# Two rows of one softmax tile loaded through GpSimd in two unequal transfers

## The chip, the cores and the metric

The kernel runs on one core of one Trainium2 chip. The metric is the time of one execution in device microseconds (us); lower is better. A time is compared with that of the kernel before in the same job, on the same chip. Times within the profile count from the span's start; the span is some 1.7 us shorter than the measured time.

## The reference

```python
batch, seq, dim = 16, 1024, 512          # x is float32, 16,384 rows of 512
x_scaled = x / 0.5
exp_x = np.exp(x_scaled - np.max(x_scaled, axis=-1, keepdims=True))
return exp_x / np.sum(exp_x, axis=-1, keepdims=True)
```

It reads 33.55 MB and writes 33.55 MB, and nothing of it is used twice.

## The kernel before

Eight tiles of 128 partitions x 16 rows x 512 (4 MB each, 32 KB per partition) go through six buffers. Sync issues the loads, VectorE (DVE) takes the row maxima and most of the scaling, ScalarE (ACT) the exponentials, two rows' scaling and the stores.

```python
G = 16
WHOLE = [(0, G)]
LOADS = [[(0, 4), (4, G)]] + [WHOLE] * 7
BUFS = 6
...
def load(c):
    if c < BUFS:
        chunks[c] = data.tile([P, G, D], fp32, name="xt")
    else:
        chunks[c] = chunks[c - BUFS]      # tiles 6 and 7 wait for stores 0 and 1
    xt = chunks[c]
    for lo, hi in LOADS[c]:
        nc.sync.dma_start(out=xt[:, lo:hi, :], in_=xr[c][:, lo:hi, :])
...
for i in range(n):
    if i + 1 < n:
        exponentials(i + 1)
    scale_vector(i)
    scale_scalar(i)
    if i + 2 < n:
        shift(i + 2)                      # row maxima; calls load(c)
    store(i)                              # nc.scalar.dma_start, 4 MB
```

Of the kernel before, what the change touches and what calls it, by code (L numbers as in the profile page):

```python
# [1 line left out]

# [4 lines left out]


@with_exitstack
def kernel(  # L10
    ctx: ExitStack,
    tc: tile.TileContext,
    x: bass.AP,
    out: bass.AP,
):
    nc = tc.nc
    fp32 = mybir.dt.float32
    P = nc.NUM_PARTITIONS
    AX = mybir.AxisListType.X
    EXP = mybir.ActivationFunctionType.Exp  # L20
    COPY = mybir.ActivationFunctionType.Copy
    MAX = mybir.AluOpType.max

    D = x.shape[-1]
    xf = x.flatten_outer_dims()
    of = out.flatten_outer_dims()
    N = xf.shape[0]




    G = 16
    C = N // (P * G)
    assert C * P * G == N
    xr = xf.rearrange("(c p g) d -> c p g d", p=P, g=G)
    outr = of.rearrange("(c p g) d -> c p g d", p=P, g=G)
    WHOLE = [(0, G)]
    LOADS = [[(0, 4), (4, G)]] + [WHOLE] * 7
    BLOCKS = [[(0, 4), (4, 8), (8, G)]] + [WHOLE] * 6 + [[(0, 8), (8, G)]]
    STORES = [WHOLE] * 8  # L40
    BMAX = 16
    BUFS = 6

    data = ctx.enter_context(tc.tile_pool(name="data", bufs=BUFS))
    stats = ctx.enter_context(tc.tile_pool(name="stats", bufs=6))

    ctx.enter_context(tc.manual_schedule())


    warm = stats.tile([P, 1], fp32, name="warm", bufs=1)  # L50
    nc.vector.memset(warm, 0.0)  # L51
    nc.scalar.activation(out=warm, in_=warm, func=EXP)  # L52

    chunks = {}
    blocks = [(c, lo, hi) for c in range(C) for lo, hi in BLOCKS[c]]
    n = len(blocks)
    biases, sums, recips = {}, {}, {}
# [5 lines that stand above are left out]
            chunks[c] = chunks[c - BUFS]  # L63
        xt = chunks[c]
        for lo, hi in LOADS[c]:
            nc.sync.dma_start(out=xt[:, lo:hi, :], in_=xr[c][:, lo:hi, :])  # L66

    def shift(i):
        c, lo, hi = blocks[i]
        if c not in chunks:  # L70
            load(c)
        b = hi - lo
        negmax = stats.tile([P, BMAX], fp32, name="negmax")
        nc.vector.tensor_reduce(  # L74
            negmax[:, 0:b], chunks[c][:, lo:hi, :], axis=AX, op=MAX, negate=True
        )
        biases[i] = stats.tile([P, BMAX], fp32, name="bias")
        nc.vector.tensor_scalar_mul(biases[i][:, 0:b], negmax[:, 0:b], 2.0)  # L78

    def exponentials(i):  # L80
        c, lo, hi = blocks[i]
        sums[i] = stats.tile([P, BMAX], fp32, name="sums")
        for g in range(hi - lo):
            row = chunks[c][:, lo + g, :]
            nc.scalar.activation(  # L85
                out=row,
                in_=row,
                func=EXP,
                bias=biases[i][:, g : g + 1],
                scale=2.0,  # L90
                accum_out=sums[i][:, g : g + 1],
            )


    def scale_vector(i):
        c, lo, hi = blocks[i]
        b = hi - lo
        k = b - b // 8
        recips[i] = stats.tile([P, BMAX], fp32, name="recip")
        nc.vector.reciprocal(recips[i][:, 0:b], sums[i][:, 0:b])  # L100
        rows = chunks[c][:, lo : lo + k, :]
        nc.vector.tensor_mul(  # L102
            rows, rows, recips[i][:, 0:k].unsqueeze(2).broadcast_to((P, k, D))
        )

    def scale_scalar(i):
        c, lo, hi = blocks[i]
        b = hi - lo
        for g in range(b - b // 8, b):
            row = chunks[c][:, lo + g, :]  # L110
            nc.scalar.activation(  # L111
                out=row, in_=row, func=COPY, scale=recips[i][:, g : g + 1]
            )

    def store(i):
        c, _, end = blocks[i]
        for lo, hi in STORES[c]:
            if hi == end:
                nc.scalar.dma_start(
                    out=outr[c][:, lo:hi, :], in_=chunks[c][:, lo:hi, :]  # L120
                )

    shift(0)
    shift(1)
    exponentials(0)
# [6 lines that stand above are left out]
            shift(i + 2)  # L132
        store(i)


# [1 line left out]
_INS = ['x']  # L137
_OUTS = [((16, 1024, 512), 'float32')]


# [23 lines left out]
```

## Time and profile before

| | before |
|---|---|
| time, median of 4 runs | 162.23 us (162.18 to 162.25) |
| span in the profile | 160.57 us |
| bytes moved | 67.13 MB, 418 GB/s over the span |
| last store issued | 147.55 us |
| its 16 increments arrive | 158.49 to 158.87 us, one at 159.71 us |

The prediction below shows the page, the windows, the timeline and the chain. Two groups of the page (line, engine, operation, output and input, count; busy time and mean; idle time before) show what DVE does in the span: maxima and scaling, one after the other, with idle time for the first two loads only.

```profile
L74 DVE TENSOR_REDUCE negmax<-xt 128x16 f32<-128x8192 f32 (+2 forms) x11 | 69.9, 6352 | 9.5 <-DMA xt<-in_x_dram 9.5
L102 DVE TENSOR_TENSOR xt<-xt,recip 128x7168 f32<-128x7168 f32 (+2 forms) x11 | 62.0, 5637 | 0.4
```

**The packets, engine by engine.** The views don't name the DMA engine of a packet, and the records don't either; they hold queue, start, duration and size. But the engines can be told apart. On one engine, a packet starts 3 or 4 ns before the recorded end of the one before it, and each transfer from Sync or ScalarE gives each engine eight data packets and then one of 4 bytes, the increment of its semaphore. With these two rules all packets of the kernel before fall into 16 chains, with none left over. I use below: the *lag* of an engine, the start of its last 4-byte packet (of store 7) less the median over the engines; and the *fetch engine*, the chain that holds the two instruction packets of 8,192 bytes. I made this after the prediction, and the chains are my own reconstruction. In the first profile of the change 2 of 2,642 packets are left over, in rows4k, one128_again and half5b1 nine. In half5, later5, early3 and sync_split more are, or the two fetches fall into two chains, and I don't use the chains there.

### The profile page before, as it was taken

The numbers are of one execution on the slowest core, as the hardware profiler recorded it, in microseconds if no ns is written. First come the engines' busy times: TensorE is split into PE (matmuls) and PEld (weight loads), VectorE is DVE, ScalarE is ACT, GpSimd is POOL, SyncE is SP. The second block draws the span as 40 slices with busy tenths as digits, with TensorE's granted clock in tenths as the row PEclk, the third lists the DMA queues.
The fourth block names the chain that finished last, engine by engine and source line by source line (L and its number), as shares of the span: only waits on it lengthen the run. The fifth ranks groups of instructions, "written<-read, shape, count | busy, mean of one in ns | idle before, by whom it ended". The sixth has DMA issues, their size and how long they took to land.

```text
span 160.6 us, 402 instructions
## 1 busy us (share of the span) xinstructions
DVE 134.6 (84%) x45; ACT 102.1 (64%) x273; POOL 0.2 (0%) x4
## 2 busy tenths in 40 slices
DVE  0507999999999999999999999999999999957000
ACT  3071549069979963998199909991899891790000
POOL 0000000000000000000000000000000000000000
DMA  5999999999999999999999999999999999999993
GB/s 182 471 400 506 400 400 498 408 392 484 424 400 384 400 457 449 400 441 465 400 424 473 408 408 492 400 392 498 416 392 490 424 392 457 457 392 449 465 392 139
DMA packets 2450, 67.13 MB, mean 418 GB/s; under 512 B 272, under 2 KB 272, under 8 KB 272
## 3 DMA queue, kind: packets, MB, share of 16 engines
q1 hardware_dynamic: 1296, 33.56, 49.3%
q10 hardware_dynamic: 1152, 33.55, 48.4%
q14 instruction: 2, 0.02, 0.0%
HBM read 33.55 MB, written 33.55 MB: 418 GB/s over the span
## 4 chain that ended last, share of the span: by engine, by line
DVE 80%; DMA 7%; ACT 4%; issue 0%; SPq 0%
DVE negmax L74 42%; DVE xt L102 36%; DMA xt<-in_x_dram 7%; ACT xt L85 4%; DVE bias L78 1%; DVE recip L100 1%; SPq L66 0%
## 5 line engine op out<-in xcount | busy, mean ns | idle before, releaser
L85 ACT ACTIVATE xt<-xt,bias 128x512 f32<-128x512 f32 x128 | 90.4, 708 | 41.7 <-DVE bias L78 41.2
L74 DVE TENSOR_REDUCE negmax<-xt 128x16 f32<-128x8192 f32 (+2 forms) x11 | 69.9, 6352 | 9.5 <-DMA xt<-in_x_dram 9.5
L102 DVE TENSOR_TENSOR xt<-xt,recip 128x7168 f32<-128x7168 f32 (+2 forms) x11 | 62.0, 5637 | 0.4
L85 ACT ACTIVATION_READ_ACCUMULATOR xt<-xt,bias 128x1 f32 x128 | 23.9, 187 | 0.0
L111 ACT ACTIVATE xt<-xt,recip 128x512 f32<-128x512 f32 x15 | 9.9, 706 | 0.0
L100 DVE RECIPROCAL recip<-sums 128x16 f32<-128x16 f32 (+2 forms) x11 | 2.4, 218 | 1.8 <-ACT xt L85 1.8
L78 DVE TENSOR_SCALAR bias<-negmax 128x16 f32<-128x16 f32 (+2 forms) x11 | 1.9, 173 | 0.4
L52 ACT ACT_TABLE_LOAD x1 | 1.3, 1283 | 0.7 <-PEq L148 0.7
L51 DVE MEMSET warm<- 128x1 f32 x1 | 0.1, 59 | 0.8 <-PEq L148 0.8
L52 ACT ACTIVATE warm<-warm 128x1 f32<-128x1 f32 x1 | 0.2, 203 | 0.0
L148 POOL MEMSET const-bfloat16-1.0<- 128x1 bf16 x1 | 0.1, 103 | 0.0
L148 POOL MEMSET const-uint8-127<- 128x1 uint8 x1 | 0.1, 103 | 0.0
L148 POOL MEMSET const-float32-1.0<- 128x1 f32 x1 | 0.1, 100 | 0.0
L148 POOL MEMSET const-float32-0.0<- 128x1 f32 x1 | 0.1, 99 | 0.2 <-issue 0.2
## 6 DMA issues: line engine op xcount, KB each, us to landing
out_dram<-xt ACTq DMA_DIRECT2D x8, 4096.0 KB, 22.8
xt<-in_x_dram SPq DMA_DIRECT2D x7, 4096.0 KB, 30.2
xt<-in_x_dram SPq DMA_DIRECT2D x1, 3072.0 KB, 11.7
xt<-in_x_dram SPq DMA_DIRECT2D x1, 1024.0 KB, 4.9
```

Source lines behind the costliest of these rows:

```text
L51: nc.vector.memset(warm, 0.0)
L52: nc.scalar.activation(out=warm, in_=warm, func=EXP)
L74: nc.vector.tensor_reduce(negmax[:, 0:b], chunks[c][:, lo:hi, :], axis=AX, op=MAX, negate=True)
L78: nc.vector.tensor_scalar_mul(biases[i][:, 0:b], negmax[:, 0:b], 2.0)
L85: nc.scalar.activation(out=row, in_=row, func=EXP, bias=biases[i][:, g : g + 1], scale=2.0, accum_out=sums[i][:, g : g + 1],)
L100: nc.vector.reciprocal(recips[i][:, 0:b], sums[i][:, 0:b])
L102: nc.vector.tensor_mul(rows, rows, recips[i][:, 0:k].unsqueeze(2).broadcast_to((P, k, D)))
L111: nc.scalar.activation(out=row, in_=row, func=COPY, scale=recips[i][:, g : g + 1])
L148: nc = _bacc.Bacc("TRN2", target_bir_lowering=False, num_devices=1)
```

## The change

Its intent, as I read it: the 16 DMA engines are the bound, and one of them is late. Part of one load is moved to GpSimd, whose transfers can be laid on other engines than Sync's, so that the late engine gets less.

```diff
+    SPLIT, TAIL = 6, 2
...
         for lo, hi in LOADS[c]:
+            if c == SPLIT and hi == G:
+                hi = G - TAIL
+                for p0, p1 in ((P - 2, P), (0, P - 2)):
+                    nc.gpsimd.dma_start(
+                        out=xt[p0:p1, hi:G, :],
+                        in_=xr[c][p0:p1, hi:G, :],
+                        max_dma_last_dim=4 * D,
+                    )
             nc.sync.dma_start(out=xt[:, lo:hi, :], in_=xr[c][:, lo:hi, :])
```

## The prediction

> **What bounds the kernel now.** I read the page first, its busy shares and its slices.
>
> ```profile
> DVE 134.6 (84%) x45; ACT 102.1 (64%) x273; POOL 0.2 (0%) x4
> ...
> DVE  0507999999999999999999999999999999957000
> ...
> DMA  5999999999999999999999999999999999999993
> ```
>
> The reader is to see that DVE is busy 84% of the span, but that the DMA row has a 9 in all slices but the first and the last. Then the windows view: busy microseconds of each engine in five stretches, with the busy share and the rate of the 16 DMA engines last.
>
> ```profile
> 0.00:45.60 45.60, 35.03 (x16) 25.09 (x67) 0.20 (x4) 1.00 0.97 414
> 45.60:71.80 26.20, 26.06 (x9) 21.41 (x59) 0.00 (x0) 1.00 1.00 420
> 71.80:115.00 43.20, 42.99 (x12) 31.18 (x85) 0.00 (x0) 1.00 1.01 436
> 115.00:147.60 32.60, 30.52 (x11) 24.43 (x65) 0.00 (x0) 1.00 1.00 433
> 147.60:160.60 13.00, 0.00 (x0) 0.00 (x0) 0.00 (x0) 1.00 0.76 328
> ```
>
> Between 45.6 and 147.6 us the DMA engines have no gap at all: 67.1 MB have to pass, and they pass at some 430 GB/s. Third, the chain of waits and the timeline around the last store (start, length, what).
>
> ```profile
> 137.56 5.76 ACT xt L85 x16
> 143.33 0.02 issue
> 143.35 0.21 DVE recip L100
> 143.56 0.02 issue
> 143.59 3.89 DVE xt L102
> ```
>
> ```profile
> 143.59 3.89 DVE L102 TENSOR_TENSOR xt<-xt,recip 128x3584 f32<-128x3584 f32 x1
> 147.55 0.34 ACTq L119 DMA_DIRECT2D out_dram<-xt  x1
> ```
>
> The last store is issued at 147.55 us. In the trace's packet records the packets of 32,768 bytes take 1.213 us, eight of them per engine and store, so 9.7 us. The first packet of store 7 starts at 148.41 us, 0.86 us after its issue. The last packets of store 6 end between 148.35 and 148.85 us on fifteen engines. So both bounds meet there with a slack of about 0.06 us: DVE delivers the last store just when most engines have finished the one before. Neither a faster DVE nor fewer bytes alone can take much off.
>
> There is one exception, and it is what the change must be about. A DMA's semaphore receives one increment from each of its 16 engines. The increments of store 7 arrive at these times (us from the span's start):
>
> ```
> 158.49 158.51 158.52 158.54 158.55 158.55 158.58 158.62
> 158.66 158.68 158.71 158.75 158.78 158.87 158.87 | 159.71
> ```
>
> Fifteen engines are done by 158.87, one comes **0.84 us later**, and the span ends 0.85 us after that one (160.57). The same late engine shows in stores 4, 5 and 6 (0.93, 0.89 and 0.86 us behind the next). It was not late in the loads of tiles 1 and 2 (the last gap is 0.09 us), and first is, by 0.41 us, in the load of tile 3, which lands at 42.4 us. What came between? The queue lines of the page have it:
>
> ```profile
> q1 hardware_dynamic: 1296, 33.56, 49.3%
> q10 hardware_dynamic: 1152, 33.55, 48.4%
> q14 instruction: 2, 0.02, 0.0%
> ```
>
> The two instruction packets inside the span are of 8,192 bytes and 0.309 us each, at 37.63 and 98.29 us. Some 60 us lie between them, about what ACT needs for 128 instructions, so I take them for ACT's instruction fetch, on one and the same engine. Two by 0.309 is 0.62 us; the 0.84 that is seen, or 1.1 against the middle of the fifteen, is more, so a fetch seems to cost about half a microsecond with what it disturbs. That these fetches are what makes one engine late is my reading; the records name no engine.
>
> **What the Trainium skill says.** "DMA: Bandwidth & Descriptors", section "Issuing engines are not separate DMA queues": transfers from Scalar, Sync and GpSimd run on the same 16 engines and interleave. The trace agrees so far: with loads and stores both in flight the windows show 436 GB/s, and 433 with stores almost alone. So GpSimd brings no bandwidth; it can only move bytes from engine to engine. How, the same page tells in "Why a DMA increments its semaphore by 16 and not by 1": a DMA runs on the largest number of engines up to 16 that divides the slowest dimension; from Sync these are the lowest-numbered ones, from GpSimd a run of consecutive engines from a round-robin cursor. It names an exception: GpSimd gives some direct copies all 16, with a sixteenth of the partitions each, rounded up. Nothing in the trace of before shows either, since all its transfers have 128 partitions. Third, "SWDGE vs HWDGE vs iDMA" on that page: descriptors of GpSimd's transfers are written to rings in SBUF by software. No run here shows that yet; POOL has only four constants in the profile.
>
> **The change part by part.** *Removed from Sync:* the load of tile 6 becomes 14 of 16 rows, so 28,672 bytes per partition. From the packet times (24,576 bytes 0.912 us, 32,768 bytes 1.213 us) that is 36.7 ns per KB, so 1.06 us a packet. Each engine has 8 partitions of it: 8 x 4,096 bytes less, 32,768 bytes, **-1.21 us** per engine.
>
> *Added through GpSimd:* 2 + 126 partitions with 2 rows of 2 KB. By the rule for the number of engines, 2 partitions go on 2 engines, one each, and 126 on 14 engines, nine each. If the cursor starts at engine 0, the small transfer takes engines 0 and 1 and moves the cursor to 2, and the large one takes 2 to 15. This is the only sense I see in loading two partitions first. The bill in bytes: two engines get back 4,096 of 32,768, fourteen get 36,864. So two engines are relieved of 28,672 bytes, 1.06 us, and fourteen have 4,096 bytes, 0.15 us, more. *Smaller rows:* the line through the three packet sizes (8,192 bytes 0.309 us) leaves about 8 ns per packet over the bytes; 18 packets instead of nothing are 0.14 us on the fourteen engines at most.
>
> *Where it falls.* Tile 6's load is issued at 69.38 us, after store 0 has landed, and lands at about 95 us; DVE wants it at 103.94. Nine microseconds are free, so the time GpSimd takes to write some 250 rows' descriptors is hidden, unless it is over that. The DMA engines have work at every moment, so what is taken off the late engine's list comes off its end: in stores 4 to 7 it is behind by the whole of its extra work. DVE gets one or two more waits before one reduction; I book 0.05 us, which the small slack may pass on to the end.
>
> *Sum, if the late engine is one of the relieved two.* Late engine: 159.71 - 1.06 = 158.65, and not before 158.49, which the last issue allows. The fourteen: 158.87 + 0.15 to 0.29 = 159.02 to 159.16. These now end the kernel: 159.71 - 159.1 = 0.6 us gained, 0.1 of which I give back for GpSimd's own waits at the end. From 162.21 that makes 161.6 to 161.7.
>
> **The rivals.** *First: the wrong engine is relieved, or none.* For it: no record names the engine, and the cursor's start is not visible. If the late engine is among the fourteen it gets 0.15 to 0.29 us more, so 162.35 to 162.5. If the exception of the skill holds, eight partitions go on each of 15 engines and six on the last; only if that one is the late one is anything won: 2 x 4,096 bytes, 0.30 us, so 161.9; otherwise 162.2 to 162.35. Against it: a tuned kernel would not have got so odd a shape (2 first, 126 then, one tile out of eight) if it hit nothing.
>
> *Second: DVE becomes the bound.* GpSimd's descriptor writing goes to SBUF while DVE reads and writes there, and any delay of DVE shifts the issue of store 7, where the slack is 0.06 us. For it: DVE has no wait from 33 us to 143 us, so nothing absorbs a delay. Against it: the last fourteen engines begin store 7 up to 0.44 us after the first could, so about 0.3 us of delay is hidden by their own lateness. A DVE delay of 1 us would undo the gain: 162.2 to 162.6.
>
> *Third: the gain is larger since a third queue gets more of the engines.* The windows speak against it: at a DMA share of 1.00 there is no empty time to fill. It would change the order of landing only.
>
> **Range and chances.** I give 60% to the relieved engine being the late one (161.5 to 161.8), 15% to a part of it (161.8 to 162.1), 25% to none or a small loss (162.1 to 162.5). The middle is 161.65, the 80% range 161.4 to 162.4. A gain of 2% would be 3.2 us; the largest lateness to be removed is 0.84 us. A loss of 2% would need a stall of DVE for over 3 us. So 0.01 faster, 0.97 same, 0.02 slower.
>
> **What would show it right or wrong.** Right: the sixteen increments of the last store lie within 0.6 us of each other with no single late one; GpSimd's queue has about 4 + 252 data packets of 2 KB; the increments of GpSimd's large transfer come from 14 engines with the data; store 7 is still issued at 147.5 to 147.7 us. Wrong: one engine still late by 0.8 us or more (rival one), by about 0.5 us (the exception, on the right engine), or all sixteen later because store 7 is issued later (rival two). I would also be wrong if GpSimd's load landed after 104 us, so that the reduction of tile 6 waited.

## The result

The changed kernel takes **162.63 us** (162.61 to 162.72, 4 runs), the one before 162.23 us (162.18 to 162.25). The ratio is 1.0026, with a 95% interval of 1.0009 to 1.0043. (A ratio is the mean time of one kernel's fast runs over that of the other's of the same rounds, so not quite the ratio of the medians.) It is "the same" at the 2% mark, but a loss of 0.4 us where I had expected a gain of 0.6, and outside my range.

The windows of the changed kernel (stretch, its length, busy time and count of DVE, ACT and POOL, clock, DMA share, GB/s):

```profile
0.00:45.60 45.60, 35.01 (x16) 25.09 (x67) 0.20 (x4) 1.00 0.97 413
45.60:71.80 26.20, 26.06 (x9) 21.39 (x59) 0.00 (x0) 1.00 1.01 419
71.80:115.00 43.20, 42.99 (x12) 31.17 (x84) 1.47 (x2) 1.00 1.00 432
115.00:147.60 32.60, 30.54 (x11) 24.45 (x66) 0.00 (x0) 1.00 1.00 430
147.60:160.90 13.30, 0.00 (x0) 0.00 (x0) 0.00 (x0) 1.00 0.81 347
```

The engines are as full as before, but in the two stretches from 71.8 us on they move 432 and 430 GB/s where they moved 436 and 433. That is a coarse sign: the kernel before has 430 in the second stretch too, in its third profile, and a later run without slowed loads (one128_again) has 428 in the first. Nothing below rests on it. DVE is not the cause; the timeline of its last work and of the last store is within 0.03 us of before:

```profile
143.61 3.89 DVE L115 TENSOR_TENSOR xt<-xt,recip 128x3584 f32<-128x3584 f32 x1
147.58 0.34 ACTq L132 DMA_DIRECT2D out_dram<-xt  x1
```

The queue lines now have a fourth queue (packets, MB, share of the engines' span):

```profile
q1 hardware_dynamic: 1296, 33.03, 48.5%
q10 hardware_dynamic: 1152, 33.55, 48.3%
q0 software_dynamic: 192, 0.52, 0.8%
q14 instruction: 2, 0.02, 0.0%
```

The 192 packets are 128 of 4,096 bytes, 32 of 8 bytes and 32 increments. So GpSimd makes packets of 4,096 bytes of the two rows, not rows of 2 KB, and fills the turns of engines without data with 8-byte packets: 14 in the small transfer, 18 (two engines by nine) in the large one. That is 2 and 14 engines with data, as predicted.

By engine, the relief worked: the fetch engine has one data packet from GpSimd where fourteen have nine, and its lag is 0.01 us in place of 1.07. Yet the increments of store 7 arrive like this:

```
158.50 | 158.85 158.88 158.89 158.90 158.94 158.95 158.98 158.99
159.07 159.13 159.17 159.23 159.30 | 159.73 159.89
```

The first is the other relieved engine, which ran 1.4 us ahead and then had to wait for the last store's issue. The rest is later by about 0.4 us, and two other engines are late. The last landing is at 159.89 us in place of 159.71, and from there to the end it takes 1.06 us in place of 0.85. These are the 0.38 us that the span grew (160.57 to 160.95).

### The profile page after: what moved, and what is told of

Same layout as the page of the kernel before. It is cut to its first block, busy times and chain, and to the rows that moved or that the text cites. A ratio compares the mean times of both kernels' runs of the same rounds, so it can differ in the third digit from the quotient of the medians.

```text
span 160.9 us, 410 instructions
## 1 busy us (share of the span) xinstructions
DVE 134.6 (84%) x45; ACT 102.1 (63%) x273; POOL 1.7 (1%) x6
## 4 chain that ended last, share of the span: by engine, by line
DVE 79%; DMA 7%; ACT 4%; issue 1%; SPq 0%
DVE negmax L87 42%; DVE xt L115 36%; DMA xt<-in_x_dram 7%; ACT xt L98 4%; DVE bias L91 1%; DVE recip L113 1%; SPq L79 0%
## 5 line engine op out<-in xcount | busy, mean ns | idle before, releaser
L74 POOL DMA_DIRECT2D xt<-in_x_dram x2 | 1.5, 736 | 71.4 <-DMA out_dram<-xt 71.4
```

What stands on the lines that cost most here:

```text
L74: nc.gpsimd.dma_start(out=xt[p0:p1, hi:G, :], in_=xr[c][p0:p1, hi:G, :], max_dma_last_dim=4 * D,)
```

## The experiments

Two theories went in. **A:** the relief is real, but costs of the GpSimd transfers, and other engines that are late, take its place. **B:** which engine is late is chance, and the fetches have nothing to do with it. The table gathers the runs whose chains I use: data packets that the fetch engine got from GpSimd, its lag, the largest lag of the others, the median engine, the last landing, and the time from it to the end of the span.

| run | fetch engine: packets, lag | others' largest lag | median engine | last landing | to the end |
|---|---|---|---|---|---|
| before | -, 1.07 | 0.24 | 158.29 | 159.71 | 0.85 |
| before_again | -, 1.03 | 0.87 | 158.40 | 159.79 | 0.85 |
| before_third | -, 1.00 | 0.23 | 158.43 | 159.79 | 0.85 |
| changed | 1, 0.01 | 0.93 | 158.62 | 159.89 | 1.06 |
| after_again | 1, -0.53 | 0.24 | 159.07 | 159.79 | 1.05 |
| after_third | 1, -0.01 | 0.23 | 159.15 | 159.86 | 1.06 |
| act_more | -, 1.52 | 0.21 | 158.22 | 160.14 | 0.85 |
| one128 | 8, 1.03 | 0.29 | 158.28 | 159.65 | 0.98 |
| one128_again | 8, 0.92 | 0.26 | 158.60 | 159.86 | 0.97 |
| large_first | 9, 1.59 | 0.29 | 158.64 | 160.59 | 1.05 |
| rows4k | 9, 1.59 | 0.27 | 158.87 | 160.81 | 1.06 |
| tail1 | 5, 1.52 | 0.46 | 158.52 | 160.40 | 1.05 |
| half | 1, 0.40 | 0.56 | 158.85 | 159.89 | 1.06 |
| half5b1 | 1, 0.90 | 0.53 | 158.35 | 159.60 | 1.13 |
| half5b4 | 1, 0.10 | 0.52 | 158.64 | 159.65 | 1.13 |
| tiny | 1, 0.91 | 0.23 | 158.25 | 159.52 | 0.98 |

**1. Both kernels again** (no edit).

> The kernel before, word for word, for a second profile. Theory A (the late engine is the one with the two instruction fetches): in the packet records, put together by engine, the same engine holds both 8,192-byte fetches and ends about 1.07 us behind the median engine; no other is over 0.3 us behind. Theory B (which engine is late is chance, different in each execution): some other engine is late, or the late one holds no fetch. Time 162.2 in both.

> The changed kernel, word for word, for a second profile. In the first one the engine with the fetches was relieved as meant (0.02 us behind the median), but two others were late: one by 0.95 us since the first store began at 47 to 51 us, before GpSimd had moved anything, and one by 0.64 us since GpSimd's transfers at 76 to 103 us. Theory A (the change causes both): both are late again by about as much, and the time is 162.6. Theory B (the first is chance): the engine late since 48 us is missing, or is late by another amount, and the span is some 0.3 us shorter, 162.3, in such an execution. The four times so far (162.61 to 162.72) speak for A.

Measured: 162.48 us (162.32 to 162.91) and 162.67 us (162.43 to 162.74), beside 162.21 us for the kernel before in the same job (162.10 to 162.75 in seven runs). So two sets of runs of the same kernel differ by 0.27 us here, and a difference of that size tells nothing. For the fetch engine my first theory holds: 1.03 us late in the kernel before, and relieved in the change. For the others it does not: in this profile of the change the engine late since 48 us is missing, as theory B of the second expectation has it, and in the kernel before two other engines are late by 0.84 and 0.87 us, since the same moment, when the first store begins. Such lateness is chance and no part of the change. In the kernel before it stays hidden behind the fetch engine.

But the time of the change did not fall with it: the *median* engine ended 0.45 us later than in the first profile. The load packets of tile 6, of 28,672 bytes, took up to 1.22 us in place of 1.06 while GpSimd's packets were in flight (half of them over 1.09 us).

**2. The change a third time.**

> The changed kernel a third time, for another profile: which of the two pictures so far it shows. The engine of the fetches is within 0.1 us of the median or ahead of it in any case. Picture 1: loads not slowed, median at 158.6, one or two engines late by 0.6 to 0.9 us. Picture 2: loads slowed by 0.3 to 0.6 us, median at 158.9 to 159.1, nobody late by over 0.3 us. Both end at 159.7 to 160.0, 162.4 to 162.8.

162.78 us (162.69 and 162.86). Picture 2: loads slowed (up to 1.32 us a packet), nobody late by over 0.23 us. So of three profiles of the change, one has late engines by chance and two have slowed loads. That the sum is about the same each time I take for coincidence; no run tests it. The loss itself came back in every job: 0.40, 0.46 and 0.60 us between the medians.

**3. More instructions for ScalarE.**

```diff
+        if 2 <= i <= 7:                       # after store(i), in the kernel before
+            for _ in range(12):
+                nc.scalar.activation(out=warm, in_=warm, func=COPY)
```

> The kernel before with 72 tiny ScalarE operations added in the idle time of ScalarE (12 after each of six tiles, about 0.2 us each, where it idles 4 us per tile). Theory A (the late engine is late through ScalarE's instruction fetches): three 8,192-byte fetches inside the span in place of two, the second earlier than 98 us, all on one engine, which ends about 1.6 us behind the median in place of 1.05; time up by about 0.5 us, to 162.7 to 162.9. Theory B (the fetches are somebody else's or don't matter): two fetches at 37 and 98 us, the late engine 1.05 us behind, 162.2 to 162.4.

162.76 us (162.68 to 162.84), ratio 1.0031 (1.0016 to 1.0046). The queue line of the page:

```profile
q14 instruction: 4, 0.02, 0.0%
```

One of the four falls at 0.04 us, before any work. The other three are at 37.66, 86.07 and 130.20 us, all in one chain, whose lag is 1.52 us. In the kernel before, 142 ScalarE instructions started between its two fetches; here 151 and 135 between the three, while VectorE's fell from 15 to 11 and 12. The added operations did not delay the last store (issued at 147.44 us). **Theory A holds.** The fetches are ScalarE's, one engine serves them, and the third costs about half a microsecond of the kernel's time, while ScalarE itself has idle time left. The cost is more than the 0.309 us of the packet: the data packet after it is long as well (1.41 to 1.59 us in place of 1.213).

**4. One transfer of 128 partitions.**

```diff
-                for p0, p1 in ((P - 2, P), (0, P - 2)):
+                for p0, p1 in ((0, P),):
```

> The last two rows of tile 6 through GpSimd as one transfer of 128 partitions: the cost of a third queue without the steering. Both theories: 8 data packets of 4,096 bytes on each of 16 engines, nobody relieved. Theory 1 (relief works but is paid for by GpSimd's queue and longer end): the engine with the fetches is late again by about 1.07 us, the end of the program takes 0.2 us longer, so 162.5 to 162.8. Theory 2 (GpSimd's packets cost nothing by themselves; the loss is only the ninth packet of the fourteen engines): 162.2 to 162.35.

> The one transfer of 128 partitions through GpSimd again, for a second profile. Theory 1 (slowed loads are a matter of chance in each execution, whichever way GpSimd's packets are dealt out): load packets of 28 KB at 1.10 to 1.25 us may show this time, with a median engine 0.3 to 0.6 us later. Theory 2 (slowed loads come only where engines hold unequal shares): none again, median at 158.3.

162.50 us (162.41 to 162.66), ratio 1.0012, and 162.60 us in the one look (state unknown, used for its profile). Eight packets on each engine and a fetch engine 1.03 and 0.92 us late: without the unequal shares, no relief. The price that this shows is the end of the program, 0.98 us in place of 0.85. No load packet of tile 6 is slowed in either profile (at most 1.08 us for 28 KB), as theory 2 of the second expectation has it; its 158.3 us for the median engine was a miss, 158.60. There the load packets had already lost some 0.35 us more than in the first profile between 44 and 52 us, before GpSimd moved anything.

**5. The large transfer first.**

```diff
-                for p0, p1 in ((P - 2, P), (0, P - 2)):
+                for p0, p1 in ((0, P - 2), (P - 2, P)):
```

> The 126 partitions first, the two partitions then. If engines are dealt out from a cursor that begins at 0, the large transfer takes the first fourteen engines and the last two are relieved. Theory 1 (the fetch engine is one of the first two, and it was relieved in the change): it now holds nine data packets, is 1.0 to 1.4 us behind the median, and the time is 162.7 to 163.0. Theory 2 (which engines are relieved doesn't matter for the time, the new late engines set it): 162.5 to 162.7, as the changed kernel.

163.48 us (163.41 to 163.67), ratio 1.0075. Theory 1: two other engines are relieved, the fetch engine has nine packets and is 1.59 us late, more than the 1.0 to 1.4 that I had put down, so the time too is above my 162.7 to 163.0. So the order of the two transfers decides who is relieved, and against this order the one in the change is worth 0.8 us.

**6. Without the limit on rows.**

```diff
-                        max_dma_last_dim=4 * D,
```

> The changed kernel without the limit of 2 KB per row, so 4 KB per partition in one row. Theory 1 (the limit doesn't matter: the packets of the change already have 4,096 bytes and take 0.159 us): the same dealing out, 14 engines with 9 packets, 2 with 1, the engine of the fetches relieved, 162.4 to 162.75. Theory 2 (the limit is what makes GpSimd choose 14 engines): all 16 engines hold 8 packets or fewer, the engine of the fetches ends 1 us late, as in the run with one transfer of 128 partitions: 162.4 to 162.7 too, but with the late engine in the records.

163.65 us (163.62 to 163.70), ratio 1.0086. Its queue line:

```profile
q0 software_dynamic: 176, 0.52, 0.8%
```

176 packets are 128 of data, 32 increments and 16 fillers (14 and 2), so the large transfer lay on all 16 engines, eight partitions each and six on one. The fetch engine was not relieved: lag 1.59 us. Load packets of tile 6 were slowed too (half of them over 1.11 us), though all engines had nearly equal shares: unequal shares, theory 2 of one128_again, are not what slows them. Theory 2 was right about the dealing out, and its time was too low. The limit, which I took for a matter of row size, is what makes the change work at all: with it the access has two dimensions behind the partitions, and GpSimd takes 14 engines.

**7. One row, uncut and cut.**

```diff
-    SPLIT, TAIL = 6, 2
+    SPLIT, TAIL = 6, 1          # tail1; half: also max_dma_last_dim=2 * D
```

> One row in place of two, so half the relief. Theory 1 (gain and cost both go with the bytes): the two relieved engines get back about 0.53 us, the fourteen lose about 0.16 in place of 0.33, the engine of the fetches ends 0.3 to 0.5 us behind the median; if no other engine is late by chance, the last landing is at 159.2 and the time 161.9 to 162.1. Theory 2 (the loss comes with the fact of a GpSimd transfer, not with its size): the loads slow down as with two rows, the median engine ends at 158.6 or later, 162.4 to 162.7.

> One row per partition again, but cut into two of 1 KB, so that the access has two dimensions behind the partitions. Theory 1 (two dimensions are what makes GpSimd take 14 engines): 9 partitions on each of 14 engines, the engine of the fetches gets back 0.53 us and is 0.3 to 0.5 us behind the median. Where the loads aren't slowed, the median ends at 158.45 and the time is 161.9 to 162.1; where they are slowed by 0.2 to 0.5 us as in four of the six profiles with GpSimd transfers on tile 6, 162.2 to 162.6. Theory 2 (dealing out is ruled by the bytes): all 16 engines used, the fetch engine late by 1.05 to 1.6 us, 162.5 or more.

tail1 took 162.96 us (162.90 to 163.24) and half 162.71 us (162.26 to 163.12). Their queue lines, tail1 first:

```profile
q0 software_dynamic: 112, 0.26, 0.4%
```

```profile
q0 software_dynamic: 128, 0.26, 0.4%
```

tail1 was meant as half the relief and was none: one row of 2 KB has one dimension, all 16 engines got three to five packets, and the fetch engine was 1.52 us late. half, with the same bytes cut into two of 1 KB, has 14 engines with five packets and two with one, and a lag of 0.40 us, inside the 0.3 to 0.5 expected. Its loads were slowed (up to 1.29 us for 30 KB, that take 1.14), and the median engine ended at 158.85 us; its time is above the 162.2 to 162.6 us of theory 1 for slowed loads. In all, with two GpSimd transfers on tile 6, loads were slowed over all engines in six of seven profiles; with one, in none of two. No run has one transfer of fewer partitions, or two halves of 64, so the number of transfers is not separated from their shape.

**8. The split on tile 3.**

```diff
-    SPLIT, TAIL = 6, 2
+    SPLIT, TAIL = 3, 2
```

> The same split on tile 3, whose load is issued in the first microseconds, when there is no store in flight. Theory 1 (part of the loss comes from the three queues being mixed at 76 to 103 us, where the loads' packets grew from 1.06 to up to 1.2 us in two of three runs): no slow load packets, the median engine ends at 158.6 as the ninth packet alone makes it, the engine of the fetches within 0.3 us of it, last landing about 159.2, 161.9 to 162.2. Theory 2 (the slow loads come from engines that run ahead of the others, whenever that is made): slow load packets here too, 162.4 to 162.7.

164.02 us (163.66 to 164.25), ratio 1.0107. GpSimd's transfers had nothing to wait for and ran from 6.7 to 19.1 us, beside the first loads, whose packets of 24 KB grew from 0.91 to over 1.1 us. The chain of waits, before and then here (start, length, what):

```profile
1.15 11.71 DMA xt<-in_x_dram
```

```profile
1.16 14.48 DMA xt<-in_x_dram
```

DVE started its second block 2.8 us later, with nothing to absorb it, and the last store was issued at 150.32 us. That says little on my two theories (a bad place for the test), but loads beside GpSimd's packets slowed here with no store in flight.

**9. Tile 5, with GpSimd held back.**

```diff
-    SPLIT, TAIL = 6, 2
+    SPLIT, TAIL = 5, 2          # half5...: 5, 1 and max_dma_last_dim=2 * D
...
+                nc.gpsimd.tensor_copy(out=hold, in_=biases[2][:, 0:1])
```

(half5b1 waits for `biases[1]` and half5b4 for `biases[4]`.)

> The split of the change on tile 5, with GpSimd held back by a tiny copy until VectorE has the third block's maxima (22 us), so that its packets meet loads only, no stores, and not the first loads that VectorE waits for. Theory 1 (the loads are slowed only where loads, stores and GpSimd's packets are in flight together): no slow load packets, median at 158.6, fetch engine within 0.1 us of it, 161.9 to 162.3. Theory 2 (GpSimd's packets slow loads wherever they run, as on tile 3): load packets grow from 1.06 and 1.21 us by 5 to 20% for some 12 us, the median engine ends 0.5 to 1 us later, 162.5 to 163.2.

> Half the relief (one row in two of 1 KB) on tile 5, held back in the same way. Theory 1: median at 158.45, fetch engine 0.3 to 0.5 us behind, 161.8 to 162.1: the best of all so far and faster than the kernel before by 0.1 to 0.4 us. Theory 2: loads slowed for the time that GpSimd's packets are in flight, 162.3 to 162.8.

> As the run with half the relief on tile 5, but GpSimd is released by the second block's maxima (15.2 us), so that its packets are done before the first instruction fetch at 37.6 us. In the run before this one the fetch fell into the slowed stretch and the fetch engine ended 0.83 us behind in place of 0.4. Theory 1 (a fetch costs double while the loads are slowed by GpSimd's packets; and half the relief is 0.53 us): the fetch engine is 0.3 to 0.45 us behind, median at 158.4 to 158.6, last landing 159.2 to 159.4, time 161.9 to 162.15. Theory 2 (the lateness there was chance when the first store begins): 162.2 to 162.6.

> The same, but GpSimd is released by the fifth block's maxima (46.2 us), so that its packets run between 49 and 75 us, with loads and stores in flight and no instruction fetch. Theory 1 (what counts is that no fetch meets GpSimd's packets): fetch engine 0.3 to 0.45 us behind, and the median 158.45 plus 0 to 0.5 us for slowed loads: 161.9 to 162.5. Theory 2 (with loads and stores mixed the loads are slowed every time): median at 158.8 or later, 162.3 to 162.6.

Measured: later5 163.21 us (ratio 1.0058), half5 162.37 us (1.0007), half5b1 162.59 us (1.0020), half5b4 162.41 us (1.0006, interval 0.9984 to 1.0028). None is faster than the kernel before. In later5, half5 and half5b1 load packets grew from 1.21 to mostly 1.3 to 1.55 us before any store had begun, as theory 2 has it. In half5 and half5b1 as much came back: in all runs with the split on tile 6 or with none, the median engine's packets lose 0.7 to 1.1 us between 44 and 52 us, when the first store begins; here they lose 0.02. (In later5 too, but there the packets had lost 1.4 us.) half5b1 speaks against my reason: no fetch met GpSimd's packets (19 to 30 us), and the fetch engine was 0.90 us late all the same.

Half a relief lowered the lag by 0.1 us there, by 0.65 in half and by 0.95 in half5b4, but the relief itself is the same in all three: by the chains, the fetch engine's GpSimd packets take 0.60 us less than the median engine's. half5b1 and half5b4 differ in what else the fetch engine lost against the median: by 0.24 us up to 5.2 us, by 0.28 us between 44 and 52 us (in half5b4 it loses 0.29 us less than the median there, in half5b1 no engine loses anything to speak of), and by 0.24 us between 52 and 104 us. Why these losses differ stays open.

half5b4 is the nearest to the aim: fetch engine 0.10 us behind. Even so the last landing came only 0.06 us earlier than before, since another engine was 0.52 us behind, and the end of the program, now with a GpSimd copy in it too, took 1.13 us.

**10. GpSimd's mere presence.**

```diff
+        if c == 6:                             # in the kernel before
+            nc.gpsimd.dma_start(out=scratch[0:2, :], in_=xr[c][0:2, 0, :])
```

> The kernel before with one transfer of 2 rows of 2 KB through GpSimd into a scratch tile that nobody reads: the price of GpSimd's queue being there at all. Theory 1 (the longer end of the program comes with the first GpSimd transfer): 0.95 to 1.06 us from the last landing to the end in place of 0.85, fetch engine 1.05 us behind, 162.3 to 162.5. Theory 2 (it comes from the two extra semaphores and waits of the split): 0.85 us, 162.2.

162.56 us (162.28 to 163.00), a wide spread, ratio 1.0020 (0.9995 to 1.0044), so the time alone tells little. The profile does: 0.98 us from the last landing to the end. One GpSimd transfer costs 0.13 us at the end; the two of the change cost 0.20.

**11. The two rows from Sync.**

```diff
-                for p0, p1 in ((P - 2, P), (0, P - 2)):
-                    nc.gpsimd.dma_start(
+                for p0, p1 in ((0, P),):
+                    nc.sync.dma_start(
```

> Last two rows of tile 6 as a transfer of their own, of 128 partitions, but from Sync. Theory 1 (the slow loads come from GpSimd's queue, not from rows of 28 KB): no slow packets, the end of the program as before (0.85 us after the last landing), the fetch engine 1.05 us behind, 162.2 to 162.35. Theory 2 (packets of 28 KB are slow by themselves): the load packets of tile 6 take 1.1 to 1.2 us, 162.5 or more.

168.23 us (167.95 to 169.38), ratio 1.0382: a miss, and no test of what I had in mind, since it made another wait. Its chain has

```profile
59.02 22.94 DMA out_dram<-xt
...
82.08 45.04 DMA xt<-in_x_dram
```

From Sync the two rows became 256 packets of 2,048 bytes, 16 on each engine, from 74.5 to 92.1 us, ahead of the other fourteen rows in Sync's queue. Each short packet takes its turn against a store's packet of 32,768 bytes. The Trainium skill says that an engine goes round its queues packet by packet ("DMA: Bandwidth & Descriptors", "Queues, rings and completion order"), and this run agrees: in those 18 us the loads got 0.5 MB, store 2 had landed by 92.5 us in place of 108.0, and tile 7 landed at 127.1 us, where DVE had wanted it at 120.6. On a queue of their own, as in the change, such packets held up nobody so: the fourteen rows of tile 6 landed at 94.9 us, as the whole tile did before (95.0).

## Why the prediction was wrong

- **The bound: right.** The DMA engines are full, DVE has no slack, and the last store is issued at 147.58 us after the change. That the fetches make one engine late, which I had only read out of the landings, is shown by act_more.
- **Which engines are relieved: right.** Two engines with one packet, fourteen with nine, and the fetch engine among the two in all three profiles of the change. The first rival (the wrong engine) fell. The skill's exception is real too, and only the limit on rows keeps the change out of it.
- **The relief: right in size.** I had 1.06 us less against 0.15 to 0.29 more for the rest, so a lag of -0.14 to -0.28 from 1.07; measured 0.01, -0.53 and -0.01. Counted in packets it is what I had: the fetch engine's GpSimd packets take 1.20 us less than the nine of the fourteen (booked: 1.06 + 0.15 = 1.21). The scatter of the lag is what else the engine lost or gained against the median.
- **"The fourteen: 158.87 + 0.15 to 0.29 = 159.02 to 159.16. These now end the kernel": this step failed**, in both its terms. *The addend* took the bytes as the only price. The bytes were priced well: on each of the fourteen GpSimd's packets take 1.42 us and the shorter load packets save 1.21, so 0.21 us more. In the first profile the median engine is 0.33 us later than before, close to it. In the other two it is at 159.07 and 159.15 us, against 158.29 to 158.43 in three profiles of before: 0.6 to 0.9 us, since load packets slowed while GpSimd's were in flight (by 0.6 and 0.7 us in sum on the median engine, between 74 and 104 us). I had said in the third rival that a third queue would change the order of landing only; I had not asked whether it changes the pace. *The base*, 158.87, was the end of fifteen engines in one execution. In the first profile of the change another engine was 0.93 us late by chance, as two were in before_again. Behind a fetch engine that is 1 us late, such things cost nothing; without it they are the end.
- **0.1 us for the end: too small.** It is 0.20 us (1.057 less 0.854), and 0.13 of it comes with any GpSimd transfer.
- **The account**, against a predicted last landing of 159.1 us: in the first profile a late engine, in the other two slowed loads, and each time 159.8 to 159.9. With 0.1 more than booked at the end, that is 0.8 to 0.9 us of the 1.0 between predicted and measured time; the rest lies within the spread of the runs.
- **"Nine microseconds are free": held, but only just.** GpSimd's large transfer landed at 103.57, 102.65 and 102.96 us in the three profiles of the change, and DVE began on tile 6 at 103.96, 103.83 and 104.05 us, without a wait. The sign "landed after 104 us" was missed by 0.4 us in the first of them.
- **The second rival** (DVE slowed by GpSimd's descriptors) fell: DVE is busy 134.6 us in both pages.
- **What I named as signs** misled in part: I had promised increments within 0.6 us of each other. They spread over 1.4 us in the first profile, also because the other relieved engine ran ahead. And "4 + 252 data packets of 2 KB" are 128 of 4 KB, so 9 for an engine and not 18. One reading of the landings was off: the 0.93 us are store 3's; stores 4, 5 and 6 have 0.90, 0.90 and 0.86.

What stays open: the mechanism by which GpSimd's packets slow the loads, why a single transfer of 128 partitions did not do it in two profiles while two transfers did in six of seven, and why the fetch engine's other losses differ so much from run to run.

## What to carry to other kernels

Where all engines of a pool are full, the latest one sets the end, so taking work off it wins only the distance to the next latest: look at the second and third over several executions before you count on it. Price a rebalancing by what the extra path does to the pace of all the others, not by its bytes; here a full microsecond of relief was real and was paid back by slower loads, chance lateness and a longer end. A setting that looks like a detail of row size can decide how a transfer is laid on the engines, so check the packet counts of the queues.

## What the Trainium skill lacked or had wrong

- "DMA: Bandwidth & Descriptors", "Why a DMA increments its semaphore by 16 and not by 1": it says that GpSimd gives "some direct copies" all 16 engines but not which. Here 126 partitions with one run each (4 KB or 2 KB) got 16 engines, and with two runs each (2 KB or 1 KB) 14; the packet counts are 176 and 112 against 192 and 128. It does not mention the 8-byte packets on engines without data either (32 in the change).
- The same page, "Issuing engines are not separate DMA queues": nothing there says that a GpSimd transfer in flight can slow the others' packets. The nearest that the page has, under "Latency and other measured facts", is a best guess that GpSimd's descriptor rings make engines 7 and 15 slower; here the packets slowed on all sixteen (by 0.3 to 0.7 us in sum on each in after_again, between 74 and 104 us). Load packets of 28 KB took up to 1.22 and 1.32 us in place of 1.06 in two of three profiles of the change, and slowed in six of seven with two GpSimd transfers on tile 6.
- The same page, "Queues, rings and completion order": it lists a queue row for the runtime's own refills, without a cost. "Runtime: NRT & Kernel Launch", "Instruction fetch mechanics", gives refills of 16 KiB and calls their cost mostly hidden. It does not mention the DMA engine that serves them: ScalarE's instruction fetches, one packet of 8,192 bytes each here, delay one of the 16 engines by about 0.5 us each (lag 1.00 to 1.07 us with two, 1.52 with three).
- On no page that I read: the end of the program grows by 0.13 us with one GpSimd transfer and by 0.20 us with the two of the change.
